# Hymba encoder block on one core: the down projection as seven block products, with sums of activations and weights stored in DRAM

## The chip, the cores and the metric

The kernel runs on one core of a Trainium2 chip. Five engines work side by side, each through its own instructions in order: TensorE (PE in the profile; its loads of stationary tiles are PEld), VectorE (DVE), ScalarE (ACT), GpSimd (POOL) and SyncE (SP), which here issues every DMA. Semaphores order them. Matmuls add into PSUM, eight banks of 128 x 512 float32; everything else lies in SBUF, 128 partitions wide, or in DRAM. The metric is the device time of one execution in microseconds (us).

## What is computed

One encoder layer on x of 1024 tokens by 1024 channels, float32: a mixing half (attention within a window, and retention in both directions), then a gated feed-forward part of depth 2816. Only the second part bears on the change:

```python
D_FF = -(-8 * D_MODEL // (3 * 256)) * 256          # 2816
...
m = rms_norm(h, ffn_norm_w[l])
h = h + (jax.nn.silu(m @ w_gate[l]) * (m @ w_up[l])) @ w_down[l]
```

## The kernel before

**Precision.** Each float32 operand is split into a rounded part and a remainder, `hi` by a ScalarE copy and `lo` by a VectorE subtraction (`split`, L871, and `split_to`, L825). A product of tiles is three matmuls, hi x hi, hi x lo and lo x hi (`passes`), each with a stationary tile of 128x128 and a moving one of 128x512. The splits of weights live in two rings of ten buffers (`wh` and `wl`, W_BUFS), the raw tiles in a ring of seven (`raw`, L877, RAW_BUFS).

**Gate and up projection.** The 2816 columns are 22 tiles of 128 (NF), taken as 11 pairs `p`. For each pair there are two units, `m` = 0 (gate) and 1 (up). A unit (`gate_up`, L954) computes a 2 x 2 block of results (two column tiles by two token halves) in seven block products rather than eight, Winograd's form: A11 B11, A12 B21, S2 T2, S1 T1, S3 T3, S4 B22 and A22 T4, where S1 to S4 are sums of weight blocks, made by VectorE (`block`, L889), and T1 to T4 are sums of activations, made once (T2 to T4 lie in the tiles `T2`, `T3` and `T4` of 16 KB a partition each, the first tiles of the pool `p2`). A product is 12 matmuls (4 depth tiles by 3 passes). Three banks take turns: `pa` collects four of the products, `pb` one, `pc` two; `snap` (L949) copies a bank out by ScalarE between two of its products, and `finish` (L930) adds, applies SiLU (gate) or multiplies with the gate's result (up). Every finished block of activations (128 columns by 512 tokens) is stored in DRAM as `Ad` (L947).

**Down projection.** For each half of the tokens all eight banks are used at once, 4 token tiles by 2 column halves. Units (half, f) run over the 22 depth tiles; each loads a block of `Ad` and two blocks of `wd` into the ring `raw`, splits the three, and issues 24 matmuls (L1009 on). The loads are written three units ahead. At the end of a half the residual `Hd`, loaded from DRAM into `hd`, is added bank by bank and stored.

**Memory and order.** The stages share memory: `mid`, with the pool `p2`, is opened where the first part's tiles lay, and closed after the gate and up stage; `pd`, whose only tile is `hd` (8 buffers of 2 KB a partition), then takes its place from the same start. Both pools say `reuse_waits="tile"`: a new tile waits for the tiles that it overlaps, not for the whole pool. The order of the instructions of each engine, SyncE's included, is set at compile time by a list scheduler: among the instructions that it holds to be ready, the one that stands first in the program goes first. So loads and splits can stand well ahead of their place in the program.

```python
    mid.close()
    pd = ctx.enter_context(tc.tile_pool(name="pd", bufs=1, reuse_waits="tile"))
    ...
        dops[u] = [split(f"d{i}{n}", raw(f"r{i}{n}", src))
                   for i, src in enumerate((Ad[f, half][:], wd[f, 0], wd[f, 1]))]
```

Of the kernel before, what the change touches and what calls it, by code (L numbers as in the profile page):

```python
# [9 lines left out]
F32 = mybir.dt.float32  # L10
F32R = mybir.dt.float32r
AF = mybir.ActivationFunctionType
ALU = mybir.AluOpType
# [3 lines left out]
P = 128  # L17
# [4 lines left out]
NF = 22  # L22
# [16 lines left out]
SOONER = {"w": -80, "exp": 10, "pass": 0}  # L39
PAIRED = (0, 4, 1, 5, 2, 6, 3, 7)  # L40
LEAD = 6
MID = {"eight": 8, "five": 5, "four": 4, "two": 2, "two_": 2, "sum": 4}
PUMP = 3
PUMP_D = 2
# [12 lines left out]
def hymba_block(ctx, tc, x, xT, cst, prm, retw, ffnw, wqkv, wkv, wout, wg, wu, wd, out):  # L57
# [3 lines left out]
    nc = tc.nc  # L61
# [31 lines left out]
    pe, act, dve, pool = (Engine(e) for e in (nc.tensor, nc.scalar, nc.vector, nc.gpsimd))  # L93
# [27 lines left out]
    dp = ctx.enter_context(tc.tile_pool(name="dp", bufs=1, space=bass.MemoryType.DRAM))  # L121
# [11 lines left out]
    def mm_ps(name):  # L133
        return pp.tile([P, 512], F32, name=name, tag="mm", bufs=MM_BUFS)

    def ax_ps(name):
        return pp.tile([P, 512], F32, name=name, tag="ax", bufs=AX_BUFS)

    def bc(ap, pos, n):
# [36 lines left out]
    A, B, C, D, O = "a", "b", "c", "d", "o"  # L176
    src = {(A, 0): wqkv[0], (B, 0): wqkv[1], (A, 1): wqkv[2], (B, 1): wqkv[3], (C, 0): wkv, (D, 0): wqkv[4],
           (O, 0): wout[0], (O, 1): wout[1]}
# [6 lines left out]
    for c in chunks:  # L185
        n = WIDE if seq else 3
# [9 lines left out]
    banks, done, blocked = {}, set(), set()  # L196
# [28 lines left out]
    def passes(ps, lh, ll, rh, rl, first, last, **kw):  # L225
        pe.matmul(ps, lh, rh, start=first, stop=False, **kw)
        pe.matmul(ps, lh, rl, start=False, stop=False, **kw)
        pe.matmul(ps, ll, rh, start=False, stop=last, **kw)
# [50 lines left out]
    def need(c, t):  # L279
        while (c, t) not in done:  # L280
            sip()
        return banks[c, t]
# [228 lines left out]
    def drain(gen):  # L511
        for _ in gen:
            pass
# [7 lines left out]
    for g in range(2):  # L521
# [4 lines left out]
        for t in range(NT):  # L526
            ps = need((A, g), t)
# [22 lines left out]
        for c in range(NT):  # L550
            ps = need((B, g), c)
# [170 lines left out]
    for t in range(NT):  # L722
        ps = need((C, 0), t)
# [41 lines left out]
    for i in range(2 * NT):  # L765
        t, kv = divmod(i, 2)
# [37 lines left out]
    def T_(name, tag):  # L804
        return p2.tile([P, 512], F32, name=name, tag=tag, bufs=MID[tag])

    H = [[None, None] for _ in range(NT)]
    Hd = [[dp.tile([P, 512], F32, name=f"Hd{t}{ch}") for ch in range(2)] for t in range(NT)]
# [16 lines left out]
    def split_to(hi, lo, v, e_lo=None):  # L825
        act.activation(hi, v, AF.Copy)
        (e_lo or dve).tensor_tensor(lo, v, f32(hi), op=ALU.subtract)
# [43 lines left out]
    def split(name, v):  # L871
        hi = wp.tile([P, 512], F32R, name=f"{name}h", tag="wh", bufs=W_BUFS)
        lo = wp.tile([P, 512], F32R, name=f"{name}l", tag="wl", bufs=W_BUFS)
        split_to(hi[:], lo[:], v[:])
        return hi, lo

    def raw(name, src):  # L877
        v = wp.tile([P, 512], F32, name=name, tag="raw", bufs=RAW_BUFS)
        nc.sync.dma_start(v[:], src)
        return v  # L880
# [2 lines left out]
    FIRST, REST = ("A11", "A12"), ("S2", "S1", "S3", "S4", "A22")  # L883
    order = [((0, m), v) for vs in (FIRST, REST) for m in range(2) for v in vs]
    order += [((p, m), v) for p in range(1, NF // 2) for m in range(2) for v in FIRST + REST]
    blocks, ready_ops = {}, {}
    prepared = [0]

    def block(unit, v):  # L889

        if (unit, v) not in blocks:
            (p, m), name = unit, f"{v}_{unit[0]}{unit[1]}"
            if v[0] == "A":
                blocks[unit, v] = raw(name, UP[m][2 * p + int(v[1]) - 1, int(v[2]) - 1])
            else:
                a, b, op = {"S1": ("A21", "A22", ALU.add), "S2": ("S1", "A11", ALU.subtract),
                            "S3": ("A11", "A21", ALU.subtract), "S4": ("A12", "S2", ALU.subtract)}[v]
                a, b = block(unit, a), block(unit, b)
                t = T_(name, "sum")
                dve.tensor_tensor(t[:], a[:], b[:], op=op)  # L900
                blocks[unit, v] = t
        return blocks[unit, v]

    def prepare(n):

        for unit, v in order[prepared[0]:prepared[0] + n]:
            if v == "A11":
                for w in ("A11", "A12", "A21", "A22"):
                    block(unit, w)
            ready_ops[unit, v] = split(f"{v}_{unit[0]}{unit[1]}", block(unit, v))  # L910
        prepared[0] += n
# [6 lines left out]
    def product(ps, unit, v, xv, first, last):  # L918
        prepare(max(0, used[0] + 1 + LEAD - prepared[0]))
        used[0] += 1  # L920
        wh, wl = ready_ops[unit, v]
        xh, xl = XOP[xv]
        for k in range(4):
            c = slice(k * P, k * P + P)
            passes(ps[:], wh[:, c], wl[:, c], xh[:, :, k, :], xl[:, :, k, :], first and k == 0, last and k == 3,
                   skip_group_check=not first)

    Ad = {(f, h): dp.tile([P, 512], F32, name=f"Ad{f}_{h}") for f in range(NF) for h in range(2)}
    SG = {}
    def finish(unit, i, j, src, add):  # L930

        p, m = unit
        n = f"{p}{m}{i}{j}"
        if m == 0:
            g = T_(f"sg{n}", "eight")
            if add is not None:
                dve.tensor_tensor(g[:], src, add, op=ALU.add)
                src = g[:]
            act.activation(g[:], src, AF.Silu)
            SG[p, i, j] = g  # L940
            return
        a = T_(f"a{n}", "four")
        if add is not None:
            dve.tensor_tensor(a[:], src, add, op=ALU.add)
            src = a[:]
        dve.tensor_tensor(a[:], src, SG[p, i, j][:], op=ALU.mult)
        nc.sync.dma_start(Ad[2 * p + i, j][:], a[:])  # L947

    def snap(name, src):  # L949
        v = T_(name, "five")  # L950
        act.activation(v[:], src[:], AF.Copy)
        return v[:]

    def gate_up(unit):  # L954
        n = f"{unit[0]}{unit[1]}"
        b1, b2 = mm_ps(f"pa{n}"), ax_ps(f"pb{n}")
        product(b1, unit, "A11", "B11", True, True)
        p1 = snap(f"p1{n}", b1)
        product(b2, unit, "A12", "B21", True, True)
        finish(unit, 0, 0, b2[:], p1)  # L960
        yield
        product(b1, unit, "S2", "T2", False, True)
        u2 = snap(f"u2{n}", b1)
        b3 = ax_ps(f"pc{n}")
        product(b3, unit, "S1", "T1", True, True)
        p5 = snap(f"p5{n}", b3)
        product(b1, unit, "S3", "T3", False, True)
        finish(unit, 1, 1, b1[:], p5)
        product(b3, unit, "S4", "B22", False, True)
        finish(unit, 0, 1, b3[:], u2)  # L970
        product(b1, unit, "A22", "T4", False, True)
        finish(unit, 1, 0, b1[:], None)
# [17 lines left out]
    go(firsts[1])  # L990
    for g in firsts:
        drain(g)
    for p in range(1, NF // 2):
        for m in range(2):
            drain(gate_up((p, m)))


    mid.close()
    pd = ctx.enter_context(tc.tile_pool(name="pd", bufs=1, reuse_waits="tile"))
    units = [(half, f) for half in range(2) for f in range(NF)]  # L1000
    dops = {}

    def prepare_down(u):
        half, f = units[u]
        n = f"{half}_{f}"
        dops[u] = [split(f"d{i}{n}", raw(f"r{i}{n}", src))
                   for i, src in enumerate((Ad[f, half][:], wd[f, 0], wd[f, 1]))]

    banks = {}  # L1009
    for u, (half, f) in enumerate(units):  # L1010
        while len(dops) < min(u + 3, len(units)):
            prepare_down(len(dops))
        (ah, al), *ws = dops[u]
        for t4 in range(4):
            for ch in range(2):
                if f == 0:
                    banks[t4, ch] = (mm_ps if 2 * t4 + ch < 3 else ax_ps)(f"pd{half}{t4}{ch}")
                ps = banks[t4, ch]
                wh, wl = ws[ch]
                c = slice(t4 * P, t4 * P + P)  # L1020
                passes(ps[:], ah[:, c], al[:, c], wh[:], wl[:], f == 0, f == NF - 1)
                if f == NF - 1:
                    t = 4 * half + t4
                    h = pd.tile([P, 512], F32, name=f"hd{t}{ch}", tag="hd", bufs=8)
                    nc.sync.dma_start(h[:], Hd[t][ch][:])
                    dve.tensor_tensor(h[:], h[:], ps[:], op=ALU.add)
                    nc.sync.dma_start(out[t * P:(t + 1) * P, ch * 512:ch * 512 + 512], h[:])


_NAMES = ["x", "xT", "cst", "prm", "retw", "ffnw", "wqkv", "wkv", "wout", "wg", "wu", "wd"]  # L1030
# [63 lines left out]
```

## Time and profile before

| | |
|---|---|
| median of 3 runs | 1220.87 us (1219.78 to 1222.08) |
| the profiled execution | 1218.89 us, of which its span is 1217.1 |
| TensorE busy | 1175.3 us (97%), 5516 matmuls |
| VectorE busy | 761.5 us (63%) |
| ScalarE busy | 527.7 us (43%) |
| GpSimd busy | 249.3 us (20%) |
| moved by DMA | 112.98 MB, mean 93 GB/s |
| gate and up stage | to 973.95 us |
| down stage | from 973.95 us to the end |

The span runs from the first to the last instruction; the profiled execution's time has what lies around it too. Times in the views count from the span's start. The idle time behind a bar in a view is the engine's own idle time just before the instruction, with the instruction that ended it. Matmuls are pipelined, so one that is shown with 0.39 us can start 0.23 us after the one before it: what a matmul costs is read from the starts.

### The profile page before, as it was taken

What the parts mean: (1) busy time and instruction counts of PE and PEld (TensorE: products, weight loads), DVE (VectorE), ACT (ScalarE), POOL (GpSimd) and SP (SyncE); (2) the same over time, 40 slices, a digit from 0 to 9 for tenths busy, and PEclk for the clock granted to TensorE, in tenths of its full rate; (3) what the DMA queues carried; (4) which work ended last, traced back from release to release, by engine and by line L of the source; (5) the groups of instructions that cost most, each with busy time, mean ns of one, the idle gap of its engine ahead of it and who ended that gap; (6) DMA issues with size and microseconds to landing.
All of it is one profiled execution on the core that took longest, in us unless ns stands there. A gap on an engine that the chain in (4) does not pass through costs nothing.

```text
span 1217.1 us, 15868 instructions
## 1 busy us (share of the span) xinstructions
PE 1175.3 (97%) x5516; PEld 955.6 (79%) x5516; DVE 761.5 (63%) x1510; ACT 527.7 (43%) x1100; POOL 249.3 (20%) x308
## 2 busy tenths in 40 slices
PE   8989998999999989979999999999999999999998
PEld 6767776778878868857888888888888888888887
DVE  6988866988899973687555555555555433343333
ACT  4744534554588762455333333333333323232331
POOL 3445714466646422120000000000000000000000
PEclk9989999999999999989999999999999999999999
DMA  8520202002100043312222223232222364457442
GB/s 287 185 65 1 67 4 69 1 18 70 36 1 10 27 126 115 108 50 84 81 87 87 78 75 91 78 96 61 78 90 84 96 217 146 149 173 257 138 149 78
DMA packets 60847, 112.98 MB, mean 93 GB/s; under 512 B 7008, under 2 KB 7520, under 8 KB 60768
## 3 DMA queue, kind: packets, MB, share of 16 engines
q1 hardware_dynamic: 60768, 111.98, 29.4%
q8 instruction: 43, 0.70, 0.2%
q14 instruction: 36, 0.29, 0.1%
HBM read 92.03 MB, written 19.92 MB: 92 GB/s over the span
## 4 chain that ended last, share of the span: by engine, by line
PE 75%; DVE 14%; POOL 4%; issue 4%; ACT 2%; DMA 1%; SPq 0%; POOLq 0%; DVEq 0%; ACTq 0%
PE pa L84 20%; PE pd L84 19%; PE pc L84 10%; PE o L84 7%; PE pb L84 5%; PE a L84 4%; PE d L84 2%; PE c L84 1%; POOL Y L84 1%; PE b L84 1%; DVE X_lo L84 1%; DVE r_t L84 1%; DVE BD L84 1%; POOL vhl L84 1%; DVE krv L84 1%
## 5 line engine op out<-in xcount | busy, mean ns | idle before, releaser
L87 POOL TENSOR_TENSOR wl<-raw,wh 128x512 fp32r<-128x512 f32 x44 | 60.0, 1388 | 70.8 <-ACT wh L87 70.3
L84 PE MATMUL o<-wh,X_hi 128*128 128x512 f32 x128 | 52.5, 410 | 2.3 <-DVE h L84 2.3
L84 PE MATMUL a<-wh,X_lo 128*128 128x512 f32 x128 | 52.0, 407 | 1.2 <-DVE X_lo L84 1.2
L84 PE MATMUL a<-wh,X_hi 128*128 128x512 f32 x128 | 51.6, 403 | 1.4 <-DVE krv L84 1.4
L84 PE MATMUL b<-wh,X_hi 128*128 128x512 f32 x128 | 52.4, 410 | 0.0
L84 PE MATMUL a<-wl,X_hi 128*128 128x512 f32 x128 | 52.0, 406 | 0.0
L84 PE MATMUL b<-wh,X_lo 128*128 128x512 f32 x128 | 51.7, 404 | 0.0
L84 PE MATMUL o<-wl,X_hi 128*128 128x512 f32 x128 | 51.5, 402 | 0.0
L84 PE MATMUL o<-wh,X_lo 128*128 128x512 f32 x128 | 51.3, 401 | 0.0
L84 PE MATMUL b<-wl,X_hi 128*128 128x512 f32 x128 | 51.1, 399 | 0.0
L84 DVE TENSOR_TENSOR S<-A,A 128x512 f32<-128x512 f32 x44 | 31.4, 715 | 1.9 <-DMA A<-in_wu_dram 1.0
L84 PEld LDWEIGHTS a<-wh,X_lo 128*128 128x128 f32 x128 | 24.8, 194 | 8.0 <-DVE X_lo L84 2.9
L84 PEld LDWEIGHTS o<-wh,X_hi 128*128 128x128 f32 x128 | 24.4, 191 | 7.7 <-DVE h L84 2.6
L87 ACT CAST wh<-raw 128x512 fp32r<-128x512 f32 x44 | 25.8, 616 | 9.9 <-PE o L84 4.8
L84 PEld LDWEIGHTS a<-wh,X_hi 128*128 128x128 f32 x128 | 24.5, 192 | 6.8 <-issue 2.0
L84 PEld LDWEIGHTS o<-wh,X_lo 128*128 128x128 f32 x128 | 24.5, 192 | 5.5
L84 PEld LDWEIGHTS a<-wl,X_hi 128*128 128x128 f32 x128 | 24.8, 194 | 5.0 <-DVE wl L84 0.4
L84 PEld LDWEIGHTS b<-wh,X_lo 128*128 128x128 f32 x128 | 24.4, 190 | 5.2
L84 PEld LDWEIGHTS o<-wl,X_hi 128*128 128x128 f32 x128 | 24.6, 192 | 5.0
L84 PEld LDWEIGHTS b<-wl,X_hi 128*128 128x128 f32 x128 | 24.5, 192 | 4.5
L84 PEld LDWEIGHTS b<-wh,X_hi 128*128 128x128 f32 x128 | 24.8, 193 | 3.9
L84 ACT ACTIVATE xr<-h 128x512 f32<-128x512 f32 x16 | 10.1, 630 | 39.1 <-DVE h L84 23.7
(2340 smaller groups left out, 3779.2 us busy)
## 6 DMA issues: line engine op xcount, KB each, us to landing
r<-in_wd_dram SPq DMA_DIRECT2D x88, 256.0 KB, 3.2
A<-in_wg_dram SPq DMA_DIRECT2D x44, 256.0 KB, 2.6
A<-in_wu_dram SPq DMA_DIRECT2D x44, 256.0 KB, 2.8
Ad<-a SPq DMA_DIRECT2D x44, 256.0 KB, 2.8
r<-Ad SPq DMA_DIRECT2D x44, 256.0 KB, 2.8
raw<-in_wqkv_dram SPq DMA_DIRECT2D x40, 256.0 KB, 2.8
xs<-in_xT_dram SPq DMA_DIRECT2D x16, 256.0 KB, 5.4
xs<-in_x_dram SPq DMA_DIRECT2D x8, 512.0 KB, 5.0
```

The lines of the kernel that those rows point to most:

```text
L84: ins = fn(*args, **kw)
L87: ins = fn(*args, **kw)
```

## The change

The down projection takes Winograd's form too. For each pair `p` the activations are a 2 x 2 block L (token halves by the pair's two depth tiles) and the weights a 2 x 2 block R (depth tiles by column halves). Seven products of such blocks replace eight, and each product is accumulated over all 11 pairs before the next begins, so the results add up in PSUM: 7 x 11 units of 4 token tiles x 3 passes.

- `left` stores seven blocks of L for each pair in DRAM (A11, A12, A22 and the sums S1 to S4; A21 itself isn't needed any more). `left_sums(p - 1)`, four VectorE operations into the tags `two` and `two_` of `p2`, stands ahead of pair p's gate unit.
- `right_sums(p - 1)` stands between pair p's gate and up units: it loads four blocks of `wd` into `raw`, makes T1 to T4 by four VectorE operations into the tag `sum` and stores them. For the last pair both stand behind the last unit.
- A down unit loads one block of L and one of R into `rd`, a new ring of ten in `pd` (its first tile now), splits both and issues 12 matmuls. Loads and splits are written five units ahead (DOWN_LEAD).
- Four banks are accumulated in a product. `keep` copies them out by ScalarE, where their content is needed twice, and adds the residual; `store` adds the last product and stores the result.

```diff
@@ -39,6 +39,9 @@
 SOONER = {"w": -80, "exp": 10, "pass": 0}
 PAIRED = (0, 4, 1, 5, 2, 6, 3, 7)
 LEAD = 6
+DOWN_LEAD = 5
+RD_BUFS = 10
+SUMS = ("two", "two_")
 MID = {"eight": 8, "five": 5, "four": 4, "two": 2, "two_": 2, "sum": 4}
 PUMP = 3
 PUMP_D = 2
@@ -883,6 +886,8 @@
     FIRST, REST = ("A11", "A12"), ("S2", "S1", "S3", "S4", "A22")
     order = [((0, m), v) for vs in (FIRST, REST) for m in range(2) for v in vs]
     order += [((p, m), v) for p in range(1, NF // 2) for m in range(2) for v in FIRST + REST]
+    SUM_OF = {"S1": ("A21", "A22", ALU.add), "S2": ("S1", "A11", ALU.subtract),
+              "S3": ("A11", "A21", ALU.subtract), "S4": ("A12", "S2", ALU.subtract)}
     blocks, ready_ops = {}, {}
     prepared = [0]
@@ -893,8 +898,7 @@
             if v[0] == "A":
                 blocks[unit, v] = raw(name, UP[m][2 * p + int(v[1]) - 1, int(v[2]) - 1])
             else:
-                a, b, op = {"S1": ("A21", "A22", ALU.add), "S2": ("S1", "A11", ALU.subtract),
-                            "S3": ("A11", "A21", ALU.subtract), "S4": ("A12", "S2", ALU.subtract)}[v]
+                a, b, op = SUM_OF[v]
                 a, b = block(unit, a), block(unit, b)
                 t = T_(name, "sum")
                 dve.tensor_tensor(t[:], a[:], b[:], op=op)
@@ -925,7 +929,35 @@
             passes(ps[:], wh[:, c], wl[:, c], xh[:, :, k, :], xl[:, :, k, :], first and k == 0, last and k == 3,
                    skip_group_check=not first)
-    Ad = {(f, h): dp.tile([P, 512], F32, name=f"Ad{f}_{h}") for f in range(NF) for h in range(2)}
+    NPAIR = NF // 2
+    Ld = {(p, v): dp.tile([P, 512], F32, name=f"L{p}_{v}") for p in range(NPAIR)
+          for v in ("A11", "A12", "A22", "S1", "S2", "S3", "S4")}
+    Rd = {(p, v): dp.tile([P, 512], F32, name=f"R{p}_{v}") for p in range(NPAIR) for v in ("T1", "T2", "T3", "T4")}
+    LA = {}
+    def left(p, v, t):
+        LA[v] = t
+        if v != "A21":
+            nc.sync.dma_start(Ld[p, v][:], t[:])
+    def left_sums(p):
+        for v, tag in (("S1", SUMS[0]), ("S2", SUMS[0]), ("S3", SUMS[1]), ("S4", SUMS[1])):
+            a, b, op = SUM_OF[v]
+            t = T_(f"L{v}_{p}", tag)
+            dve.tensor_tensor(t[:], LA[a][:], LA[b][:], op=op)
+            left(p, v, t)
+    def right_sums(p):
+        r = {(i, j): raw(f"R{i}{j}_{p}", wd[2 * p + i - 1, j - 1]) for i, j in ((1, 2), (1, 1), (2, 2), (2, 1))}
+        t = {v: T_(f"R{v}_{p}", "sum") for v in ("T1", "T2", "T3", "T4")}
+        for v, a, b in (("T1", r[1, 2], r[1, 1]), ("T2", r[2, 2], t["T1"]), ("T3", r[2, 2], r[1, 2]),
+                        ("T4", r[2, 1], t["T2"])):
+            dve.tensor_tensor(t[v][:], a[:], b[:], op=ALU.subtract)
+            nc.sync.dma_start(Rd[p, v][:], t[v][:])
     SG = {}
     def finish(unit, i, j, src, add):
@@ -944,7 +976,7 @@
             dve.tensor_tensor(a[:], src, add, op=ALU.add)
             src = a[:]
         dve.tensor_tensor(a[:], src, SG[p, i, j][:], op=ALU.mult)
-        nc.sync.dma_start(Ad[2 * p + i, j][:], a[:])
+        left(p, f"A{j + 1}{i + 1}", a)
     def snap(name, src):
         v = T_(name, "five")
@@ -990,41 +1022,83 @@
     go(firsts[1])
     for g in firsts:
         drain(g)
-    for p in range(1, NF // 2):
-        for m in range(2):
-            drain(gate_up((p, m)))
+    for p in range(1, NPAIR):
+        left_sums(p - 1)
+        drain(gate_up((p, 0)))
+        right_sums(p - 1)
+        drain(gate_up((p, 1)))
+    left_sums(NPAIR - 1)
+    right_sums(NPAIR - 1)
     mid.close()
     pd = ctx.enter_context(tc.tile_pool(name="pd", bufs=1, reuse_waits="tile"))
-    units = [(half, f) for half in range(2) for f in range(NF)]
+    PRODUCTS = (("A11", "R11"), ("A12", "R21"), ("S2", "T2"), ("S1", "T1"), ("S3", "T3"), ("S4", "R22"), ("A22", "T4"))
+    units = [(v, p) for v in PRODUCTS for p in range(NPAIR)]
     dops = {}
     def prepare_down(u):
-        half, f = units[u]
-        n = f"{half}_{f}"
-        dops[u] = [split(f"d{i}{n}", raw(f"r{i}{n}", src))
-                   for i, src in enumerate((Ad[f, half][:], wd[f, 0], wd[f, 1]))]
-    banks = {}
-    for u, (half, f) in enumerate(units):
-        while len(dops) < min(u + 3, len(units)):
-            prepare_down(len(dops))
-        (ah, al), *ws = dops[u]
-        for t4 in range(4):
-            for ch in range(2):
-                if f == 0:
-                    banks[t4, ch] = (mm_ps if 2 * t4 + ch < 3 else ax_ps)(f"pd{half}{t4}{ch}")
-                ps = banks[t4, ch]
-                wh, wl = ws[ch]
-                c = slice(t4 * P, t4 * P + P)
-                passes(ps[:], ah[:, c], al[:, c], wh[:], wl[:], f == 0, f == NF - 1)
-                if f == NF - 1:
-                    t = 4 * half + t4
-                    h = pd.tile([P, 512], F32, name=f"hd{t}{ch}", tag="hd", bufs=8)
-                    nc.sync.dma_start(h[:], Hd[t][ch][:])
-                    dve.tensor_tensor(h[:], h[:], ps[:], op=ALU.add)
-                    nc.sync.dma_start(out[t * P:(t + 1) * P, ch * 512:ch * 512 + 512], h[:])
+        (lv, rv), p = units[u]
+        srcs = Ld[p, lv], Rd[p, rv] if rv[0] == "T" else wd[2 * p + int(rv[1]) - 1, int(rv[2]) - 1]
+        dops[u] = []
+        for v, src in zip((lv, rv), srcs):
+            r = pd.tile([P, 512], F32, name=f"d{lv}{v}_{p}", tag="rd", bufs=RD_BUFS)
+            nc.sync.dma_start(r[:], src if v[0] == "R" else src[:])
+            dops[u].append(split(f"e{lv}{v}_{p}", r))
+    def down(v, bs, first):
+        for p in range(NPAIR):
+            u = units.index((v, p))
+            while len(dops) < min(u + DOWN_LEAD, len(units)):
+                prepare_down(len(dops))
+            (lh, ll), (rh, rl) = dops[u]
+            for i in range(4):
+                c = slice(i * P, i * P + P)
+                passes(bs[i][:], lh[:, c], ll[:, c], rh[:], rl[:], first and p == 0, p == NPAIR - 1,
+                       skip_group_check=not first)
+    def keep(n, bs, t0, ch):
+        out_ = []
+        for i in range(4):
+            h = pd.tile([P, 512], F32, name=f"{n}h{i}", tag="hd", bufs=8)
+            nc.sync.dma_start(h[:], Hd[t0 + i][ch][:])
+            v = pd.tile([P, 512], F32, name=f"{n}{i}", tag="keep", bufs=8)
+            act.activation(v[:], bs[i][:], AF.Copy)
+            dve.tensor_tensor(h[:], h[:], v[:], op=ALU.add)
+            out_.append(h)
+        return out_
+    def store(bs, hs, t0, ch):
+        for i in range(4):
+            t = t0 + i
+            h = hs[i]
+            dve.tensor_tensor(h[:], h[:], bs[i][:], op=ALU.add)
+            nc.sync.dma_start(out[t * P:(t + 1) * P, ch * 512:ch * 512 + 512], h[:])
+    b1 = [(mm_ps if i < 3 else ax_ps)(f"da{i}") for i in range(4)]
+    down(PRODUCTS[0], b1, True)
+    h11 = keep("h11", b1, 0, 0)
+    b2 = [ax_ps(f"db{i}") for i in range(4)]
+    down(PRODUCTS[1], b2, True)
+    store(b2, h11, 0, 0)
+    down(PRODUCTS[2], b1, False)
+    h12 = keep("h12", b1, 0, 1)
+    b3 = [ax_ps(f"dc{i}") for i in range(4)]
+    down(PRODUCTS[3], b3, True)
+    h22 = keep("h22", b3, 4, 1)
+    down(PRODUCTS[4], b1, False)
+    store(b1, h22, 4, 1)
+    down(PRODUCTS[5], b3, False)
+    store(b3, h12, 0, 1)
+    h21 = []
+    for i in range(4):
+        h = pd.tile([P, 512], F32, name=f"h21{i}", tag="hd", bufs=8)
+        nc.sync.dma_start(h[:], Hd[4 + i][0][:])
+        h21.append(h)
+    down(PRODUCTS[6], b1, False)
+    store(b1, h21, 4, 0)
 _NAMES = ["x", "xT", "cst", "prm", "retw", "ffnw", "wqkv", "wkv", "wout", "wg", "wu", "wd"]
```

## Rows read from the trace of the kernel before

**Rows 1.** The page: busy time of each engine, share of the span, instructions.
```profile
PE 1175.3 (97%) x5516; PEld 955.6 (79%) x5516; DVE 761.5 (63%) x1510; ACT 527.7 (43%) x1100; POOL 249.3 (20%) x308
```
**Rows 2.** Windows: stretch, length; busy by engine; granted clock, DMA share, GB/s.
```profile
583.00:760.00 177.00, 177.00 (x763) 143.09 (x762) 94.78 (x144) 65.33 (x111) 0.00 (x0) 1.00 0.27 82
...
1000.00:1208.00 208.00, 208.00 (x920) 172.22 (x919) 74.30 (x118) 61.49 (x110) 0.00 (x0) 1.00 0.48 151
```
**Rows 3.** Chain that ended last: start, us, what; end of the gate stage on.
```profile
971.19 2.76 PE pa L84 x12
973.95 234.61 PE pd L84 x1035
```
**Rows 4.** Waits of TensorE from 541 us on: total, times, longest.
```profile
PE pa L84 <- DVE X_lo L84: 1.7, 1, 1.7
PE pa L84 <- DVE T L84: 0.3, 1, 0.3
```
**Rows 5.** Timeline of TensorE: start, us, instruction; first and last down matmul.
```profile
973.56 0.39 PE L84 MATMUL pa<-T,A_101l 128*128 128x512 f32 x1
973.79 0.39 PE L84 MATMUL pd<-d_0h 128*128 128x512 f32 x1
...
1212.92 0.39 PE L84 MATMUL pd<-d_21h,d_21l 128*128 128x512 f32 x1
```
**Rows 6.** Groups of VectorE, gate stage: busy, mean ns | idle before, releaser.
```profile
L84 DVE TENSOR_TENSOR S<-A,A 128x512 f32<-128x512 f32 x36 | 24.9, 691 | 0.9
...
L84 DVE TENSOR_TENSOR a<-pc,u 128x512 f32<-128x512 f32 x10 | 6.9, 692 | 8.7 <-PE pc L84 8.7
```
**Rows 7.** Timeline of VectorE: last operation of attention, and the gate stage's end.
```profile
448.86 0.69 DVE L84 TENSOR_TENSOR q7yA<-q7yA,q71o 64x512 f32<-64x512 f32 x1
...
972.44 0.68 DVE L84 TENSOR_TENSOR a<-a,sg 128x512 f32<-128x512 f32 x1
973.99 0.69 DVE L84 TENSOR_TENSOR a<-pa,sg 128x512 f32<-128x512 f32 x1 [0.87 <-PE pa L84]
974.60 0.68 DVE L84 TENSOR_TENSOR d_3l<-r,d_3h 128x512 fp32r<-128x512 f32 x1
```
**Rows 8.** Waits of ScalarE in the gate stage (one of many alike).
```profile
ACT S_81h L84 <- PE pa L84: 5.5, 3, 2.2
```
**Rows 9.** Groups of ScalarE: bank copies in the gate stage, splits in the down stage.
```profile
L84 ACT ACTIVATE u<-pa 128x512 f32<-128x512 f32 x20 | 11.6, 582 | 0.0
...
L84 ACT ACTIVATE d_10h<-r 128x512 fp32r<-128x512 f32 x6 | 3.5, 622 | 7.5 <-PE pd L84 7.5
```
**Rows 10.** The page: DMA issues, count, KB each, median us to landing.
```profile
r<-in_wd_dram SPq DMA_DIRECT2D x88, 256.0 KB, 3.2
```
**Rows 11.** DMA issues from 1000 to 1208 us, same columns.
```profile
hd<-Hd SPq DMA_DIRECT2D x8, 256.0 KB, 5.3
```
**Rows 12.** Windows, columns as in rows 2: between the two halves of down.
```profile
1091.00:1107.00 16.00, 16.00 (x72) 13.27 (x71) 9.56 (x16) 5.03 (x9) 0.00 (x0) 1.00 0.95 322
```
**Rows 13.** Timeline of SyncE: start, us from first issue to last, tile, count.
```profile
436.05 12.96 SPq L816 DMA_DIRECT2D xr<-in_x_dram  x5
...
973.15 1.88 SPq L947 DMA_DIRECT2D Ad<-a  x2
975.31 0.33 SPq L879 DMA_DIRECT2D r<-in_wd_dram  x1
975.74 1.35 SPq L1025 DMA_DIRECT2D hd<-Hd  x3
...
1090.13 5.41 SPq L1027 DMA_DIRECT2D out_dram<-hd  x8
```
**Rows 14.** Timeline of TensorE at the start of the gate stage.
```profile
537.68 0.79 PE L84 MATMUL pa<-X_hi,A_00h 128*128 128x512 f32 x1 [3.71 <-ACT X_hi L84]
...
541.17 0.80 PE L84 MATMUL pa<-X_lo,A_00h 128*128 128x512 f32 x1 [1.72 <-DVE X_lo L84]
...
546.03 0.63 PE L84 MATMUL pb<-X_lo,A_00h 128*128 128x512 f32 x1
```
**Rows 15.** Windows, columns as in rows 2: the same place.
```profile
541.00:546.00 5.00, 4.83 (x11) 3.84 (x12) 4.56 (x10) 0.28 (x2) 0.93 (x1) 0.50 0.13 52
```

## The prediction

> **What bounds the kernel now.** I read the page's busy time first: TensorE is busy 97% of the span, VectorE 63% [rows 1]. A share over the whole span hides stages, so next come the stretches: in the gate and up stage TensorE is busy all 177 of 177 us at the full granted clock, VectorE 95 and ScalarE 65; in the down stage it is 208 of 208 against 74 and 61 [rows 2]. The chain of waits agrees: from 973.95 it is one unbroken piece of down matmuls [rows 3]. After 541 us TensorE's waits come to 2.0 us in all [rows 4]. So both stages are paid by the matmul, and a matmul that disappears is worth its spacing, as long as the operands of the others still come in time.
>
> **The matmuls removed.** Now: 44 units (2 token halves x 22 depth tiles) of 4 x 2 x 3 matmuls, 1056. Then: 7 products x 11 pairs x 4 x 3, 924. The first starts at 973.79, the last at 1212.92, which is 239.1 / 1055 = 0.2267 us each [rows 5]. Stationary and moving tiles keep their shapes and lie contiguous as before, so I keep the spacing: 132 x 0.2267 = **-29.9 us**. A unit of 12 then takes 2.72 us, the stage 209.5. What follows the last matmul, an addition and a store, stays.
>
> **Sums in the gate and up stage.** For each of 11 pairs VectorE gets 4 sums of activations and 4 of weights, each like "S<-A,A", 0.691 us [rows 6]: 5.5 us in 39. Its share goes from 95/177 = 54% to some 68%. TensorE depends on VectorE most tightly where a bank is read out before it is accumulated upon one product (2.8 us) later. The tightest kind of these additions, "a<-pc,u", finds VectorE idle for 8.7 / 10 = 0.9 us before it [rows 6]: it starts as soon as the bank is complete and ends 0.7 later. A run of 4 sums in front of it (2.4 us at the 0.6 spacing of back-to-back ones [rows 7]) would make that 3.1, 0.3 too late. I take **0**, as every such addition has a gap ahead of it. Bound above: 0.3 us at each of 20 joints, or 1.2 where VectorE also waits out part of a weight load, so 6 to 24. Below zero is excluded, since TensorE has no wait there to give back [rows 2].
>
> SyncE's queue gets per pair 3 more stores of activations (seven blocks, A21 not among them, for four), 4 weight loads and 4 stores of weight sums: 11 DMAs of 256 KB in 39 us, 74 GB/s on top of 82 [rows 2]. The gate weights queue behind stores that wait for sums, some 3 us late. Cover: ScalarE's splits wait for TensorE to release a buffer, not for data [rows 8], so ten products (28 us) of operands stand ready. Without it those 3 us would count at each of 20 joints.
>
> **Feeding the down stage.** A unit now needs two loads, two ScalarE splits and two VectorE splits in 2.72 us; before, three of each in 5.44. Splits: 2 x 0.62 on ScalarE [rows 9], 2 x 0.69 on VectorE [rows 7]. Two issues on SyncE, 0.33 each [rows 13]. Bytes: 154 + 16 loads and 16 stores of 0.262 MB, 48.8 MB in 209 us, 233 GB/s; in the middle of the old stage the queues moved 322 GB/s with TensorE busy throughout [rows 12]. All of it fits in 2.72 us and runs five units ahead, so **0**. The copies out of the banks (4 x 0.58 on ScalarE [rows 9], 4 additions of 0.69) lie beside a whole other product of 29.9 us, after which alone bank set b1 is written again. Without that cover they would cost 2.3 us at each of three joints.
>
> **The join of the stages: where a stall goes in.** Now the first loads for down land in the buffers `raw`, which live through both stages, so their splits are done before 973.8 and no gap shows [rows 5]. After the change they land in `rd`, in the pool `pd`, which is opened when `mid` is closed and lies where `mid` lay. The row nearest to this is `hd`, today's only tile in `pd`. Its memory is the first 16 KB of `mid`, that of T2, last read by the third product of the last unit, four products (11 us) before 973.95. Yet the first `hd` load is issued at 975.74, right behind the last store out of `mid` [rows 13]. So I read: loads into `pd` are queued behind the last instruction that uses `mid`. That will be the store of S4 = A12 - S2, whose A12 is the very last finish. Working forward on today's rows: A21's product ends at 972.44 + 0.68; S1, S2, A12, S3, S4 follow at 0.6 each from 973.05, so S4 ends near 976.2 (975.3 if it follows A12 at once) [rows 7]. Store, then two loads 0.43 apart [rows 13], the second issued at 977.05. It lands 3.2 us later [rows 10], 980.25; its ScalarE split takes 0.63, 980.9. TensorE would have started at 973.8: a gap of 7.1 us (6.2 with the early S4, 9.2 with the 5.3 us that `hd` takes to land beside other traffic [rows 11]). I take **+7.0**, as the first two transfers have the queues to themselves. The granted clock adds to it: after waits of 3.7 and 1.7 us near 540 it is 0.50 (1.2 GHz) up to 546, and 12 matmuls stand 0.43 apart [rows 14, 15] instead of 0.23; 12 x 0.2 = **+2.4**. Bounds: 0, if the clock holds, to twice this. Later units need 0.52 MB each, 1.6 us at 322 GB/s, less than 2.72, so nothing else is late.
>
> The Trainium skill, "DMA: Bandwidth & Descriptors", section "Latency and other measured facts", says that HBM access takes 0.2 us on average but 2 us under high load. Ten loads go out at once at the join, so by that rule the second one would land some 1.8 us later, the gap would be an estimated 8.8 us and the time some 1202. The row for `hd`, 5.3 against 3.2 us, leans the same way.
>
> **Sum.** On the profiled execution (1218.9; its span is 1217.1): 1218.9 - 29.9 + 0 + 0 + 7.0 + 2.4 = 1198.4. The median shown is 1220.9, 2.0 above that execution, so the forecast is **1200 us**.
>
> **Rivals.** (1) No stall. Loads into a new pool can run before the old one is done: `xr`, the first loads into `mid`, began at 436.05 [rows 13] while VectorE still worked for attention at 448.86 [rows 7]. If `rd` does that, its tiles, in the memory of T2 and T3, are free 5.6 us before 973.95, and load and split are hidden: 1200.4 - 9.4 = **1191**. Against it stands the place of `hd`. (2) Sums delay the gate stage by 6 to 24 us, as costed: 1206 to 1224, say **1210**. For it: VectorE works in order, and a late weight load would block all behind it. Against it: 36 sums that wait for loads now cost VectorE 0.9 us of idle time in all [rows 6]. (3) Slower: the one queue holds the loads back. It also carries stores that wait for VectorE at the ends of products, and loads behind them start late. If a unit's load and two splits stood in line instead of running ahead, it would take 3.2 + 2 x 0.62 = 4.4 us instead of 2.72, 77 x 1.7 = +131 us: **1331**. It decides from (29.9 - 9.4) / 77 = 0.27 us exposed per unit. Against it: at 1090 the queue stood 5.4 us over eight such stores [rows 13] and TensorE did not stop [rows 12]. That the matmuls are not fewer is excluded by the loops.
>
> **Chances.** Forecast 0.62 (own range 1195 to 1206), rival 1 0.17, rival 2 0.15, rival 3 0.04, and 0.02 for a smaller loss that cancels the gain. Reaching to rival 1 and into rival 2, the range is 1190 to 1211. A measurement can tell some 0.2% (2.4 us) from nothing; faster by more 0.94, the same 0.02, slower 0.04.
>
> **What would show it.** TensorE instructions 5516 - 132 = 5384; 924 down matmuls 0.2267 apart with no wait inside; one wait of 6 to 9 us at the first of them, released by a ScalarE split, with the clock at 0.50 after it; 68% of VectorE in the gate stage and no new wait of TensorE there. The forecast is wrong if the first `rd` load is issued before the last gate product ends, if a gate unit takes more than 19.5 us, or if the spacing in the down stage leaves 0.2267 under 233 GB/s.

## The result and the profile after

The changed kernel takes **1201.23 us** (median of 4 runs, 1199.28 to 1202.74), the kernel before beside it 1220.96 us (4 runs, 1219.78 to 1222.08): a ratio of 0.9838, 95% interval 0.982 to 0.9856. The forecast was 1200 us. The profiled execution of the changed kernel took 1201.98 us, its span 1199.9.

First the busy times of the whole span, to be held against [rows 1]:

```profile
PE 1150.6 (96%) x5384; PEld 935.2 (78%) x5384; DVE 833.7 (69%) x1632; ACT 549.5 (46%) x1134; POOL 249.4 (21%) x308
```

TensorE has 132 instructions fewer, and VectorE's share went from 63 to 69%. Next a window in the gate and up stage and one inside the down stage (columns as in [rows 2]: busy time and count of TensorE, its weight loads, VectorE, ScalarE, GpSimd, then granted clock, DMA share, GB/s):

```profile
586.00:763.00 177.00, 177.00 (x763) 143.09 (x762) 116.80 (x183) 65.52 (x111) 0.00 (x0) 1.00 0.51 164
...
1016.00:1190.00 174.00, 174.00 (x769) 144.15 (x768) 93.72 (x148) 76.49 (x134) 0.00 (x0) 1.00 0.66 211
```

In the gate stage VectorE is busy 66% of the time instead of 54, and the queues move 164 GB/s instead of 82 (156 were forecast); TensorE is busy throughout at the full clock (2.4 GHz), as before. In the down stage it is busy in all 174 of 174 us.

TensorE's waits from 541 us on (waited for, us in total, times, longest), the view of [rows 4]:

```profile
PE da L87 <- ACT eA11R_0h L87: 7.0, 1, 7.0
PE pa L87 <- ACT X_hi L87: 3.7, 1, 3.7
PE pa L87 <- DVE X_lo L87: 1.7, 1, 1.7
PE pa L87 <- DVE T L87: 0.3, 1, 0.3
```

One wait is new, the first line: the first down matmul waits 7.0 us for a split of ScalarE. The 3.7 us are old: they are the wait at 537.68 in [rows 14]. This execution ran some 2.5 us later there and to the end of the gate stage (last gate matmul at 976.10 against 973.56), so that the matmul behind that wait, at 540.34, reaches into the window. How the new wait comes about stands in the chain of waits (start, us, what):

```profile
974.50 0.70 DVE a L87
...
975.83 0.73 DVE LS L87 x2
...
977.04 0.69 DVE a L87
...
977.75 0.70 DVE LS L87
...
978.47 0.32 SPq L944
...
978.89 3.29 DMA dA11A<-L_A
...
982.20 0.63 ACT eA11A_0h L87
...
982.84 0.64 ACT eA11R_0h L87
...
983.52 33.06 PE da L87 x132
...
1016.58 29.92 PE db L87 x132
1046.50 29.92 PE da L87 x132
```

The last gate matmul starts at 976.10. Behind it VectorE multiplies (`a`) and subtracts (`LS`, which is S4), SyncE stores S4 at 978.47 and only then issues the first load of the down stage, the load takes 3.29 us, and ScalarE splits both operands one behind the other. From 983.52 on there are only matmuls, 132 to a product, 29.92 us each; the first product takes 33.06. SyncE's timeline shows the order of stores and loads:

```profile
977.75 0.32 SPq L944 DMA_DIRECT2D L_A<-a  x1
978.47 0.32 SPq L944 DMA_DIRECT2D L_S<-LS  x1
978.89 0.40 SPq L1047 DMA_DIRECT2D dA11A<-L_A  x1
979.38 0.41 SPq L1047 DMA_DIRECT2D dA11R<-in_wd_dram  x1
```

And VectorE's groups in the gate stage (count, busy us, mean ns, idle time before them and what ended it), beside [rows 6] and, in the last line, a group of the kernel before that is not shown there:

```profile
L87 DVE TENSOR_TENSOR S<-A,A 128x512 f32<-128x512 f32 x36 | 24.7, 687 | 0.3
...
L87 DVE TENSOR_TENSOR a<-pc,u 128x512 f32<-128x512 f32 x10 | 6.9, 692 | 9.0 <-PE pc L87 9.0
...
L87 DVE TENSOR_TENSOR sg<-pa,p 128x512 f32<-128x512 f32 x10 | 6.8, 684 | 1.1 <-PE pa L87 1.1
...
L84 DVE TENSOR_TENSOR sg<-pa,p 128x512 f32<-128x512 f32 x10 | 6.9, 692 | 16.6 <-PE pa L84 16.6
```

`a<-pc,u`, which the prediction calls the tightest kind, still finds VectorE idle 0.9 us before it. By the kernel it isn't a tight one: in `gate_up` the bank `pc` is not written again in the unit once this addition has read it. The tight ones are `sg<-pa,p` and `a<-pa,p`, between whose reading of `pa` and the next product on `pa` only one other product lies. The gap before `sg<-pa,p` is one of those that the sums have taken, 16.6 us down to 1.1; what that left TensorE stands under "sums3" below.

### The profile page after: what moved, and what is told of

It reads as the page before. It is cut to its first block, busy times and chain, and to the rows that moved or that the text cites. A ratio compares the mean times of both kernels' runs of the same rounds, so it can differ in the third digit from the quotient of the medians.

```text
span 1199.9 us, 16078 instructions
## 1 busy us (share of the span) xinstructions
PE 1150.6 (96%) x5384; PEld 935.2 (78%) x5384; DVE 833.7 (69%) x1632; ACT 549.5 (46%) x1134; POOL 249.4 (21%) x308
## 4 chain that ended last, share of the span: by engine, by line
PE 74%; DVE 14%; POOL 4%; issue 4%; ACT 2%; DMA 1%; SPq 0%; POOLq 0%; DVEq 0%; ACTq 0%
PE pa L87 20%; PE pc L87 10%; PE da L87 10%; PE o L87 7%; PE dc L87 5%; PE pb L87 5%; PE a L87 4%; PE db L87 2%; PE d L87 2%; PE c L87 1%; POOL Y L87 1%; PE b L87 1%; DVE X_lo L87 1%; DVE krv L87 1%; DVE r_t L87 1%
## 5 line engine op out<-in xcount | busy, mean ns | idle before, releaser
L87 PE MATMUL o<-wh,X_hi 128*128 128x512 f32 x128 | 52.3, 408 | 2.2 <-DVE h L87 2.2
L87 PE MATMUL a<-wh,X_hi 128*128 128x512 f32 x128 | 51.8, 405 | 2.5 <-DVE krv L87 2.5
L87 PE MATMUL b<-wh,X_hi 128*128 128x512 f32 x128 | 53.3, 416 | 0.0
L87 PE MATMUL a<-wh,X_lo 128*128 128x512 f32 x128 | 51.9, 406 | 1.1 <-DVE X_lo L87 1.1
L87 PE MATMUL b<-wh,X_lo 128*128 128x512 f32 x128 | 52.4, 409 | 0.0
L87 PE MATMUL b<-wl,X_hi 128*128 128x512 f32 x128 | 52.0, 406 | 0.0
L87 PE MATMUL a<-wl,X_hi 128*128 128x512 f32 x128 | 51.9, 405 | 0.0
L87 PE MATMUL o<-wl,X_hi 128*128 128x512 f32 x128 | 51.5, 402 | 0.0
L87 PE MATMUL o<-wh,X_lo 128*128 128x512 f32 x128 | 51.5, 402 | 0.0
L87 DVE TENSOR_TENSOR S<-A,A 128x512 f32<-128x512 f32 x44 | 31.3, 712 | 1.2 <-DMA A<-in_wu_dram 0.9
L87 PEld LDWEIGHTS a<-wh,X_hi 128*128 128x128 f32 x128 | 24.6, 192 | 7.8 <-issue 2.9
L87 PEld LDWEIGHTS a<-wh,X_lo 128*128 128x128 f32 x128 | 24.7, 193 | 7.7 <-DVE X_lo L87 2.4
L87 PEld LDWEIGHTS o<-wh,X_hi 128*128 128x128 f32 x128 | 24.5, 192 | 7.9 <-DVE h L87 2.7
L87 PEld LDWEIGHTS b<-wh,X_lo 128*128 128x128 f32 x128 | 24.9, 195 | 5.4
L87 ACT ACTIVATE sg<-sg 128x512 f32<-128x512 f32 x33 | 20.9, 633 | 18.0 <-DVE sg L87 18.0
L87 PEld LDWEIGHTS o<-wh,X_lo 128*128 128x128 f32 x128 | 24.5, 191 | 5.4
L87 PEld LDWEIGHTS a<-wl,X_hi 128*128 128x128 f32 x128 | 24.8, 194 | 5.0 <-DVE wl L87 0.3
L87 PEld LDWEIGHTS b<-wl,X_hi 128*128 128x128 f32 x128 | 25.0, 195 | 4.5
L87 PEld LDWEIGHTS o<-wl,X_hi 128*128 128x128 f32 x128 | 24.5, 191 | 5.0
L87 PEld LDWEIGHTS b<-wh,X_hi 128*128 128x128 f32 x128 | 25.1, 196 | 4.0
```

Source lines behind the costliest of these rows:

```text
L87: ins = fn(*args, **kw)
```

## The experiments

All start from the changed kernel except "sums_only". Inserted lines shift the later line numbers of a kernel by a few (L87 becomes L88, L1047 becomes L1050 or L1051).

### Loads that don't wait for the old memory

```diff
+RAW_UNITS = 3
...
-            r = pd.tile([P, 512], F32, name=f"d{lv}{v}_{p}", tag="rd", bufs=RD_BUFS)
-            nc.sync.dma_start(r[:], src if v[0] == "R" else src[:])
+            if u < RAW_UNITS:
+                r = raw(f"d{lv}{v}_{p}", src if v[0] == "R" else src[:])
+            else:
+                r = pd.tile([P, 512], F32, name=f"d{lv}{v}_{p}", tag="rd", bufs=RD_BUFS)
+                nc.sync.dma_start(r[:], src if v[0] == "R" else src[:])
```

> Edit: the loads of the first three units of the down stage go into the buffers that live through both stages instead of the ones in the new memory region. Theory (loads into the new region are queued behind the last store out of the old one): these six loads go out before the last gate product ends, the wait of 7.03 us ahead of the first down matmul is gone, the clock doesn't fall, so 1201.2 - 7.2 - 3.0 = 1191 us. If the fourth unit is late, a wait of 0 to 2 us shows ahead of unit 3. Rival (something else holds the join: the banks, or VectorE busy with the last sums): the wait stays near 7 us and the time near 1201.

1191.34 us (4 runs, 1190.41 to 1192.48; ratio to the kernel before 0.9764, interval 0.9748 to 0.978). On TensorE's timeline the last gate matmul and the first down matmul:

```profile
974.75 0.39 PE L88 MATMUL pa<-T,A_101l 128*128 128x512 f32 x1
974.98 0.39 PE L88 MATMUL da<-eA11R_0h,eA11A_0h 128*128 128x512 f32 x1
```

They stand 0.23 us apart, the ordinary spacing, and the clock stays at 1.00. So the whole distance between 1201 and 1191 is the join. This version beats both: by the medians it is 29.4 us below the kernel before and 9.9 us below the changed one (1191.34 / 1201.23 = 0.9918).

The same with the first unit alone (`RAW_UNITS = 1`):

> Edit: only the first unit of the down stage is loaded into the buffers that live through both stages; the second and later ones go into the new region. Theory (the first load into the new region leaves at its old place behind the store of S4, in the queue with a load into each of two buffers ahead of a split): no wait at the first down matmul; unit 1 is due 2.7 us later and ready at some 983.5 on the time axis of the kernel after, against 979.0, so TensorE waits 4 to 5 us there, with the clock low after it: 1201.2 - 2.7 = 1198 to 1199 us. Rival (both loads go out earlier than that, since fewer stand in the queue): no wait, 1191.

1198.52 us (4 runs, 1197.52 to 1199.1). TensorE's new wait sits ahead of unit 1:

```profile
PE da L88 <- ACT eA11R_1h L88: 4.0, 1, 4.0
```

One unit is worth its 2.7 us of cover and no more; two further units close the rest.

### What holds the first load: the memory, the queue, or neither

```diff
     if p == NPAIR - 1 and v == "S4":
+        for _ in range(4):
+            dve.tensor_tensor(t[:], t[:], t[:], op=ALU.max)
     left(p, v, t)
```

> Edit: four more operations of VectorE on S4 of the last pair (each the maximum of S4 with itself, which leaves it as it is), ahead of its store. Theory (the first load of the down stage goes out behind the store of S4, the last one from the old region, though it reads another tile): the store, the first load and the wait at the join move by 4 x 0.6 to 0.7 us, so the wait is 9.5 to 9.9 us instead of 7.03 and the time some 1204 us. Rival (the load waits for the last reader of the memory it lands in, or for the last matmul): the wait stays near 7.0 and the time near 1201.

1202.75 us (4 runs, 1200.76 to 1204.82). SyncE's timeline:

```profile
978.78 0.32 SPq L944 DMA_DIRECT2D L_S<-LS  x1
979.19 0.38 SPq L1050 DMA_DIRECT2D dA11A<-L_A  x1
```

And TensorE's wait for it:

```profile
PE da L87 <- ACT eA11R_0h L87: 9.6, 1, 9.6
```

The wait grew by 2.6 us, with the four operations (2.87 us on VectorE's timeline): the load goes out 0.41 us behind the store of S4, whenever that is. The median grew by only 1.5 us, but the four runs lie 4 us apart, so that can't be told from 2.6; in the one execution with a trace the clock took 1.1 us less than in that of the changed kernel (table below). The run doesn't tell whether the load stands behind the store in the queue or waits for the memory. That does the next one, which moves the last pair's stores to another queue:

```diff
-            nc.sync.dma_start(Ld[p, v][:], t[:])
+            (nc.gpsimd if p == NPAIR - 1 else nc.sync).dma_start(Ld[p, v][:], t[:])
```

> Edit: the stores of the last pair's activations and sums (A11, A22, A12, S1 to S4) are issued by GpSimd, which has nothing to do there, instead of SyncE; the loads of the down stage still land in the new memory region. Theory A (the first loads wait only because they stand behind the store of S4 in SyncE's queue; of the memory they need no more than the last reader of T2): they go out before the last gate product ends, the wait at the join is gone, 1191 us. Theory B (the prediction's reading taken literally: the new region waits for the last user of the old one, whatever queue that is on): the first load still goes out after the store of S4, the wait stays 6.5 to 8 us, 1200 to 1203 us.

1196.35 us (4 runs, 1196.0 to 1196.69), between the two. The first loads on SyncE's timeline:

```profile
964.84 0.32 SPq L1047 DMA_DIRECT2D dA11A<-L_A  x1
970.41 0.33 SPq L1047 DMA_DIRECT2D dA11R<-in_wd_dram  x1
```

GpSimd's timeline has the store of S4, 13 and 8 us later, and the chain of waits has the products S2 x T2 and S3 x T3 of the last unit:

```profile
978.20 0.54 POOL L944 DMA_DIRECT2D L_S<-LS  x1 [0.19 <-issue]
...
962.05 2.76 PE pa L87 x12
...
967.62 2.77 PE pa L87 x12
```

S2 x T2 ends at 964.81 and S3 x T3 at 970.39, and a load leaves 0.03 and 0.02 us behind each: `rd` lies in the memory of T2 and T3, and these are their last readers. (That the second load's buffer is one in the memory of T3 is read from the times.) So the memory was free well before S4; what held the loads in the changed kernel was the order of SyncE's queue. Why the scheduler sets loads into `pd` behind the stores there, while "raw3" has its first load into `raw` out at 947.43, no run shows. But a wait of 3.0 us is left, and VectorE's timeline shows for what:

```profile
977.21 0.69 DVE L87 TENSOR_TENSOR LS<-a,LS 128x512 f32<-128x512 f32 x1
977.82 0.68 DVE L87 TENSOR_TENSOR eA11A_0l<-dA11A,eA11A_0h 128x512 fp32r<-128x512 f32 x1
978.43 0.68 DVE L87 TENSOR_TENSOR eA11R_0l<-dA11R,eA11R_0h 128x512 fp32r<-128x512 f32 x1
```

TensorE's wait, by its view of waits:

```profile
PE da L87 <- DVE eA11R_0l L87: 3.0, 1, 3.0
```

The split stands behind S4 on VectorE, which works in order too. Of my two theories the first was right on what holds the load and wrong on the time: with the queue cleared, the next queue in line was late.

### What the clock costs

```diff
+    idle2 = ax_ps("idle2")
+    for _ in range(30):
+        pe.matmul(idle2[:], X_hi[:, 0, 0, :], X_hi[:, 0:4, 0, :], start=True, stop=True)
     b1 = [(mm_ps if i < 3 else ax_ps)(f"da{i}") for i in range(4)]
```

> Edit: thirty matmuls whose result nothing uses, into a bank of their own, between the last gate matmul and the first down matmul; nothing else. They are extra work in the time in which TensorE waits. Theory (the clock falls to half because TensorE waited): the gap is filled by some 6.8 us of matmuls, the first product of the down stage takes 29.9 us and not 33.06, so 1201.2 - 3.0 = 1198 us, with the first down matmul still starting near 983.5. Rival (the clock is low for another reason, the burst of ten loads or the change of stage): first product 33 us, time 1201.

1197.78 us (4 runs, 1195.92 to 1198.89), no run of it as slow as the fastest of the changed kernel. The window from 984 to 986 in the changed kernel:

```profile
984.00:986.00 2.00, 2.00 (x5) 1.46 (x5) 0.85 (x2) 0.53 (x2) 0.00 (x0) 0.50 0.98 348
```

And in this one:

```profile
984.00:986.00 2.00, 2.00 (x10) 1.66 (x9) 1.52 (x3) 1.64 (x3) 0.00 (x0) 1.00 1.06 375
```

Ten matmuls instead of five, at 2.4 instead of 1.2 GHz, with the DMA burst the same: the burst and the change of stage are not what lowers the clock, TensorE's standing still is. The matmuls that do nothing give 3 us back without a shorter wait.

One execution of each kernel, from the start of the last gate matmul to the first matmul of the second product (30.17 us in "raw3", where nothing is lost). "Late" is how much later than 0.23 us the first late down matmul starts after the one before it; what is left is the clock.

| kernel | last gate matmul | second product | distance | over 30.17 | late | clock |
|---|---|---|---|---|---|---|
| raw3 | 974.75 | 1004.92 | 30.17 | 0 | 0 | 0 |
| changed | 976.10 | 1016.42 | 40.32 | 10.15 | 7.19 | 2.96 |
| warm (filled) | 975.69 | 1012.99 | 37.30 | 7.13 | 7.01 | 0.12 |
| s4long | 973.51 | 1015.31 | 41.80 | 11.63 | 9.78 | 1.85 |
| poolq | 975.57 | 1010.39 | 34.82 | 4.65 | 3.14 | 1.51 |
| raw1 | 974.70 | 1012.21 | 37.51 | 7.34 | 4.19 | 3.15 |
| sums3 (below) | 974.37 | 1018.92 | 44.55 | 14.38 | 12.15 | 2.23 |

### The sums in the gate stage

The kernel before, with the sums, their loads and their stores added and the old down projection kept:

```diff
+        left(p, f"A{j + 1}{i + 1}", a)
...
-    for p in range(1, NF // 2):
-        for m in range(2):
-            drain(gate_up((p, m)))
+    for p in range(1, NPAIR):
+        left_sums(p - 1)
+        drain(gate_up((p, 0)))
+        right_sums(p - 1)
+        drain(gate_up((p, 1)))
+    left_sums(NPAIR - 1)
+    right_sums(NPAIR - 1)
```

> Edit, on the kernel before: the sums of activations and of weights with their loads and stores are added to the gate stage, and nothing reads them; the down stage is the old one with 1056 matmuls. Theory (sums lie beside the gate products): 1221 us, within 2 us of the kernel before, VectorE at some 66% in the gate stage, no new wait of TensorE. Rival (the second of the prediction): TensorE waits 0.3 to 1.2 us at some twenty joints, 1227 to 1245 us.

1221.18 us (10 runs, 1219.02 to 1222.95) against 1220.73 (13 runs); ratio 1.0003, interval 0.9993 to 1.0012. The gate window:

```profile
586.00:763.00 177.00, 177.00 (x764) 143.14 (x763) 116.69 (x183) 64.93 (x110) 0.00 (x0) 1.00 0.51 170
```

VectorE's 66% cost nothing, and TensorE's waits from 541 us on are the 1.7 and 0.3 us of [rows 4]. A gate unit takes 19.52 us in the kernel before (first matmuls of two units at 583.39 and 602.91) and in the changed one (585.93 and 605.45). How much cover is left was asked with three times the work in the changed kernel:

```diff
             dve.tensor_tensor(t[:], LA[a][:], LA[b][:], op=op)
+            for _ in range(2):
+                dve.tensor_tensor(t[:], t[:], t[:], op=ALU.max)
...
             dve.tensor_tensor(t[v][:], a[:], b[:], op=ALU.subtract)
+            for _ in range(2):
+                dve.tensor_tensor(t[v][:], t[v][:], t[v][:], op=ALU.max)
```

> Edit: each sum of activations and of weights is followed by two operations of VectorE on it that leave it as it is, so that the sums cost VectorE three times as much, some 16 us in 39 instead of 5.5; its share in the gate stage goes from 66% to some 93%. At the join S4 is ready some 5 us later, so the wait there is 12 us instead of 7. Theory A (the slack of the stage covers what fits into it on average): no other wait of TensorE, some 1206 us. Theory B (second rival of the prediction, the order on VectorE counts: an addition behind a run of sums is late): twenty joints lose 0.3 to 6 us each, 1212 to 1326 us.

1204.57 us (4 runs, 1204.23 to 1205.36). The gate window:

```profile
586.00:763.00 177.00, 177.00 (x764) 143.18 (x763) 159.59 (x259) 64.43 (x110) 0.00 (x0) 1.00 0.49 158
```

Two of VectorE's groups in the gate stage, and the timelines of VectorE and TensorE around one addition of the tight kind:

```profile
L87 DVE TENSOR_TENSOR a<-pc,u 128x512 f32<-128x512 f32 x10 | 6.9, 691 | 9.0 <-PE pc L87 9.0
...
L87 DVE TENSOR_TENSOR sg<-pa,p 128x512 f32<-128x512 f32 x10 | 6.8, 683 | 0.0
...
754.16 0.69 DVE L87 TENSOR_TENSOR RT<-R,R 128x512 f32<-128x512 f32 x1
754.76 0.68 DVE L87 TENSOR_TENSOR sg<-pa,p 128x512 f32<-128x512 f32 x1
...
754.08 0.39 PE L87 MATMUL pa<-T,S_50l 128*128 128x512 f32 x1
757.12 0.63 PE L87 MATMUL pa<-T,A_50h 128*128 128x512 f32 x2
```

TensorE's only new wait:

```profile
PE da L87 <- ACT eA11R_0h L87: 12.0, 1, 12.0
```

VectorE is busy 159.59 / 177 = 90%, and TensorE still runs the whole window. The gap before `a<-pc,u` is untouched; the extra operations went into those before other additions. `sg<-pa,p` has none left: it stands right behind weight sums, starts 0.29 us after the product on `pa` has ended (754.08 + 0.39) and ends 1.68 us before the next one on that bank begins (757.12). In the kernel before, the same addition started 0.11 us after its product and had 1.85 us to spare. A gate unit still takes 19.52 us (584.20 to 603.72). The loss is at the join alone: S4 is ready 5 us later, the wait 12.0 instead of 7.0. Theory A holds.

### Feeding the down stage

`RD_BUFS = 2` instead of 10:

> Edit: two buffers for the down stage's loads instead of ten, so a unit's loads wait until the splits of the unit before are done. Theory (third rival of the prediction: a load and its splits in line cost more than a unit's 2.72 us): one unit takes 0.4 + 2.8 to 3.2 + 2 x 0.63 = 4.5 to 4.9 us, 77 x 1.8 to 2.2 = 140 to 170 us more, 1340 to 1370 us. Rival (the split operands stand five units ahead and cover it): 1201.

1325.8 us (2 runs, 1324.6 and 1326.99), under the range I gave. A unit costs 2.72 + (1325.8 - 1201.2) / 77 = 4.34 us. One unit's turn in the chain of waits:

```profile
1107.63 2.58 DMA dS2S<-L_S
...
1110.31 0.64 ACT eS2S_7h L87
1110.95 0.02 issue
1110.97 0.70 DVE eS2S_7l L87
1111.68 0.02 issue
1111.69 2.68 DMA dS2S<-L_S
```

Here load, ScalarE split and VectorE split stand in line, 4.06 us for this unit. I had added 0.4 us for the issue, which lies inside the load's 2.58, and taken the load itself at 2.8 to 3.2. With `RD_BUFS = 4`:

> Edit: four buffers for the down stage's loads instead of ten, two units' worth. With two buffers a unit took 4.34 us (1325.8 us in all). Theory (a load and its splits in line take some 4.3 us, and two units of them run side by side, so 2.2 us a unit against TensorE's 2.72): no wait inside the down stage beyond the start, 1201 to 1204 us. Rival (third of the prediction: the one queue issues loads in order and stands still whenever the next buffer isn't free, so that stores and loads behind it are late): waits of over 0.27 us at many units, 1222 us or more.

1201.15 us (4 runs, 1200.82 to 1201.94), the wait at the join 7.2 us and none after it. Two units in flight are enough; six of the ten buffers buy nothing.

## Why the prediction was right

**The matmuls removed.** Right: 5384 instructions, and products of 132 matmuls in 29.92 us, which is 0.2267 each. The spans of the profiled executions close: 1199.9 - 1217.1 = -17.2, made of -29.9 for the matmuls, +7.2 for the gap, +3.0 for the clock, and +2.5 by which this execution came later to the gate stage. This last part isn't the change's: the lag is there before the first sum (the matmul at 541.17 in [rows 14] starts at 543.83 here), and the last gate matmul of the seven executions in the table above lies anywhere between 973.51 and 976.10. The first three parts alone give -19.7, the difference of the medians.

**The gate sums at 0.** Right, and shown alone ("sums_only"), but the reason given was read from the wrong addition. The 0.9 us that VectorE is idle before `a<-pc,u` say nothing of TensorE, which doesn't come back to that bank within the unit; for the addition that is tight, `sg<-pa,p`, "every such addition has a gap ahead of it" doesn't hold after the change. The 0 came true because VectorE gets to it in time all the same: the sums ahead of it delayed it by only 0.2 us out of 1.85, even with 24 operations in the place of 8 ("sums3"). That nothing longer fell there was not argued, and in that the 0 was luck. The bound of 6 to 24 us had no case in these kernels; VectorE's in-order work becomes a cost only at the end of the stage, where nothing covers it.

**Feeding at 0.** Right: no wait of TensorE in the stage. The traffic inside it is 211 GB/s, not 233. The decision point of the third rival can be seen from both sides: two buffers put the loads in line and give 4.34 us a unit and 1325.8 us, where that rival had 4.4 and 1331; four buffers bring it back to 1201.15.

**The join.** Mechanism right, route nearly. Forecast +7.0, measured a wait of 7.03; that it came so near is luck in part, as two errors cancel. On the axis of this execution, 2.54 later at the last gate matmul, the steps were to be: S4 done at 978.7 (978.4 in the chain: 977.75 + 0.69), second load issued at 979.6 (979.38), then 3.2 and one split of 0.63. The chain instead goes over the first load, issued 0.49 earlier and 3.29 us under way, and two splits in line, 1.27; the earlier issue and the second split about cancel. The row on `hd` was read a little too strictly, since a load into `raw` stands between the last store and it (975.31 in [rows 13]). The sentence that loads into `pd` are queued behind the last instruction that uses `mid` was right in what it gave, and true of SyncE's queue only: "poolq" shows that the memory itself comes free tile by tile, 5.6 us before the last gate product ends for the second of the two, as rival 1 had it. Rival 1's mechanism for the memory is real, then, and its time of 1191 is what "raw3" gives; it needs the loads ahead of the store on SyncE and the splits ahead of S4 on VectorE.

By the Trainium skill, "DMA: Bandwidth & Descriptors", section "Latency and other measured facts", the second load would have been late under the burst, with an estimated gap of 8.8 us. The trace doesn't show that for the first two loads (3.29 us, both split by 983.47). Later loads of the burst do take longer: the fourth, issued at 980.34, is split only from 985.60 on, 5.3 us later, when nothing waits for it yet. The same page, section "Issuing engines are not separate DMA queues", says that issuing DMAs from several engines saves only the time to initiate them. "poolq" differs here: moving seven stores to GpSimd let the first load out at 964.84 instead of 978.89, since what was saved is the wait of the issuing engine for S4.

**The clock.** +2.4 was forecast, 2.96 measured: the first unit's twelve matmuls take from 983.52 to 989.11, 5.59 us, instead of 2.72. Other executions lost 1.5 to 3.2 us (table above), so the size was hit in part by luck. "warm" shows the cause: the same late start with TensorE kept busy costs 0.12 us. The Trainium skill, "TensorE: Matmul & The Clock Gate", section "Part 1: The HAM clock gate", says that the throttled clock is the default and activity releases it; the trace agrees (0.50 against 1.00 in the window above).

**Range and rivals.** 1201.23 lies 1.2 us from the forecast and inside its own range. Rival 2 and rival 3 did not occur.

## What to carry to other kernels

When a stage is emptied into memory and the next one reads it back, work out the join on its own: list for the first operand the queue of every engine that it passes, for each queue stands behind the last work of the old stage, and clearing one only shows the next. Give the first few loads of the new stage buffers that don't depend on the old one, early enough in the queue of the loads and of the splits; here six buffers that were there already were worth 10 us. Find the tight step by asking when the bank that it reads is written next, not by how long its engine is idle before it. A sum off the critical path costs nothing as long as the tight steps still end in time, but the last one at the end of the stage is paid in full.

## What was not expected of the hardware

The loss to the clock doesn't follow the length of the wait: 1.51 us after a wait of 3.0, 3.15 after 4.0, 2.96 after 7.0, 1.85 after 9.6 and 2.23 after 12.0. Each is one execution; what sets the size can't be told from these runs.

A load goes out 0.41 us behind a store of another tile in the same queue, although by "poolq" its own memory had been free for some 13 us: SyncE's queue doesn't look past an instruction that waits.
